# The low part of block 2's mixer weights: a subtraction, or a transfer that adds onto the negated high part

## The chip, the cores and the metric

The kernel runs on one core of one Trainium2 chip. A core has five engines with a queue each, worked off strictly in order: TensorE (PE: matmuls, and PEld: its weight loads), VectorE (DVE), ScalarE (ACT), GpSimd (POOL) and SyncE (SP). SP, ACT and POOL can issue DMA transfers; engines wait for each other by semaphores. The metric is the device time of one execution in microseconds (us), lower is better.

## The reference

The reference runs three transformer blocks over 512 tokens of width 1024 in float32. The change touches the mixers of the second block, which has two layers:

```python
for layer in range(DEPTH_2):
    h = rms_norm(x, g_mix[layer])
    proj = jnp.einsum('bsd,dc->bsc', h, w_in[layer])
    qa, ka, va, iq, ik, iw, qb, kb, vb = jnp.split(proj, split_points, axis=-1)
    # rotary embedding of qa, ka, iq, ik, qb, kb
    # dsa_mixer(qa, ka, va, iq, ik, iw) and diff_mixer(qb, kb, vb, ...), side by side
    # x += their outputs @ w_out[layer]; then a gated feed-forward part
```

The sparse mixer (dsa) scores all keys for each query with eight small index heads, keeps the 128 largest scores of each query, and attends over those keys alone; the differential mixer (diff) subtracts one softmax map from another. All products are in float32.

## The kernel before

**Exact products in two parts.** TensorE takes a reduced form of float32 (fp32r). Each operand is therefore split into a high part, its rounded value, and a low part, the rest, and a product is made of three matmuls: high by high, high by low, low by high (`mm3`, lines 348 to 352, where the weights stand still and 512 tokens stream by; lines 333 to 335 in `tok_steps`, where the tokens stand still and the weights' columns stream by).

**A piece of weights.** `load_piece` (lines 276 to 285) brings [128, n] of a weight, n up to 1024 columns: SP issues the transfer into `wraw` (four buffers), ACT casts it into `whi` (line 283), and DVE subtracts the high part from the weights into `wlo` (line 284); `whi` and `wlo` have three buffers each. A new cast into a buffer waits until TensorE has done the products of the piece three before. A piece of 1024 columns in `mm3` gives TensorE 24 matmuls.

**A layer of block 2** (`block2`, lines 880 to 1126) runs in these stages, at these times in the first layer's profile. The entrance (672 to 740 us): three index pieces of the weight `win`, each followed by the rotary embedding; then `wtA` (three pieces of 792, 792 and 528 columns; the values of half the sparse heads and the index weights, all four token tiles at once); then the first pair of query and key pieces of `win`, while the index scores (tiles `is` and `isc`, lines 927 to 942) are made. The selection stretch (740 to 840): DVE picks the largest scores eight at a time (`top8`, lines 922 to 925, tiles `m` and `isc`), TensorE does `wtC` (four pieces, the differential mixer's values) and the units of attention. The plan of attention (to 960): a written string, PLAN, sets the order of head pairs and query tiles; at each step `feed` puts a few matmuls of the coming projections in between (the other 14 query and key pieces, then `wtB`, two pieces, the values of the other sparse heads, then half of `wout` in eight pieces of 512 columns). The rest of `wout` and the feed-forward part follow.

**The rotary embedding** (`rope`, lines 867 to 878) is made for 19 tiles of a layer: ACT copies the product out of PSUM (line 871) and issues transfers that swap the halves of each head (line 874, ACT's queue), POOL multiplies by one table (line 875), DVE by the other (line 876), POOL adds (line 877).

**The order of the work.** A scheduler takes the program and writes each engine's queue from its own estimate of durations; an engine then works its queue in that order. So an instruction that moves to another engine changes the places of others too.

In what follows `p` is a product's PSUM tile, `is` and `s` the index and attention scores, `rope` the buffers of the embedding, `stile` a softmax tile.

Of the kernel before, what the change touches and what calls it, by code (L numbers as in the profile page):

```python
# [12 lines left out]
F32 = mybir.dt.float32  # L13
F32R = mybir.dt.float32r
I32 = mybir.dt.int32
AF = mybir.ActivationFunctionType
ALU = mybir.AluOpType
# [3 lines left out]
P = 128  # L21
# [9 lines left out]
# ---------------------------------------------------------------- host layout  # L31
def kpieces(w):
    """[K, M] -> [M/128, 128, K/128 * 128]: one block of columns per row, the contraction on partitions."""
    k, m = w.shape
    a = w.reshape(k // P, P, m // P, P).transpose(2, 1, 0, 3)
    return np.ascontiguousarray(a).reshape(m // P, P, k)


def kmajor(w):
    """[K, N] -> [128, K/128 * N]."""  # L40
    k, n = w.shape
    return np.ascontiguousarray(w.reshape(k // P, P, n).transpose(1, 0, 2)).reshape(P, -1)


def colvec(v):
    """[n * 128] -> [128, n]."""
# [24 lines left out]
def prep(i):  # L71
# [22 lines left out]
    # block 1  # L94
# [43 lines left out]
    # block 2  # L138
# [31 lines left out]
    # block 3  # L170
# [27 lines left out]
# ---------------------------------------------------------------- device code  # L198
class Build:
    def __init__(self, tc, aps, offs, ctx):  # L200
        self.tc, self.nc, self.aps, self.offs = tc, tc.nc, aps, offs
        self.ctx = ctx
        self.uid = 0
        self.sb = ctx.enter_context(tc.tile_pool(name="sb", bufs=1))
# [15 lines left out]
    def t512(self, dt=F32, name="t"):  # L220
        """A [128, 512] slot, taken in program order and given back with free()."""
# [15 lines left out]
    def set_ring(self, **kinds):  # L237
        """Slots that short-lived tiles of a kind go round; 0 gives them back."""
# [13 lines left out]
    def banks(self, **kinds):  # L252
        """Which PSUM banks each kind of product goes round."""
# [22 lines left out]
    # weights: one DMA of [128, n <= 1024], then the exact two-part split  # L276
    def load_piece(self, ap):
        nc = self.nc
# [7 lines left out]

    def split(self, src, name="s", tiles=None):
        """src [128, n] F32 (SBUF or PSUM) -> hi, lo."""
# [6 lines left out]
    def lin_T(self, ap, xs, tag="mm", piece=None):  # L295
        """ap [128, K] (one block of 128 output rows); xs: list of (hi, lo) per k-tile -> PSUM [128, 512]."""
        return last_of(self.lin_steps(ap, xs, tag, piece))

    def lin_steps(self, ap, xs, tag="mm", piece=None):
        """lin_T, a k-tile a step; the last step gives the result."""  # L300
# [16 lines left out]
    def tok_steps(self, ap, n, xs, done, wide=1):  # L317
        """ap [128, 8 * n]: tokens on partitions, PSUM [128, n] per token tile to done(tt, ps)."""
# [22 lines left out]
    def scaled(self, o, scale, name):  # L341
        """o * scale in two parts."""
# [4 lines left out]
    def mm3(self, out, w, x, start=True, stop=True):  # L347
        """out (+)= w.T @ x, either operand in two parts."""
# [5 lines left out]
    def scores(self, q, k, qt, masks, mx, sm):  # L354
        """Per half: exp(max - (q.k + mask)) with its row sums; q carries the turned sign."""
# [19 lines left out]
    def turned(self, t, qt):  # L375
        """[queries, keys] -> the blocks of keys on partitions, [128, block, 128 queries]."""
# [10 lines left out]
    def rsqrt(self, y, v, pool=False):  # L387
        """y = v ** -0.5 on small [128, n] tiles; v is SBUF and positive."""
# [17 lines left out]
    def bcast_cols(self, col_of_tt, tag="at"):  # L406
        """[128 tokens, 128 (broadcast)] stationary per token tile -> PSUM [128, 512] rows."""
# [5 lines left out]
    def bcast_pairs(self, cols, tag="at"):  # L413
        """cols [128 tokens, 4, 2] -> PSUM [128 = (2, 64), 512]."""
# [4 lines left out]
    # sums of squares of the residual stream, and what follows from them  # L419
# [19 lines left out]
    def col_sums(self, *accs):  # L439
        """-> PSUM [128 tokens, 4]: sums over the partitions."""  # L440
# [9 lines left out]
    def stat_end(self, st):  # L450
        """-> [128 tokens, 4]: 1 / rms"""
# [13 lines left out]
    def norm_in(self, x, g, hi, lo):  # L465
        """hi + lo = x * g, g a per-partition column."""
# [6 lines left out]
    # ------------------------------------------------------------ block 1  # L473
    def block1(self, x, B, first, g_next, stats):
# [36 lines left out]
        # the overlapping windows of the compressed keys and values, position pairs on partitions  # L511
# [99 lines left out]
        # relative bias strips, sign turned: strip[p, h, c] = -bias[bucket(p + 384 - c)], masked where negative  # L611
# [30 lines left out]
        # the two halves of the spatial gating unit, in parts that go between others  # L642
# [28 lines left out]
        # q / k norms per head  # L671
# [16 lines left out]
        # compressed branch probabilities, transposed to [(r, n), q]  # L688
# [1057 lines left out]
```

## Time and profile before

| | |
|---|---|
| Time, median of 3 runs | 3123.69 us (3121.01 to 3126.1) |
| Span of the profiled execution | 3123.8 us (nothing around it is shown) |
| Mean granted TensorE clock | 0.979 of full speed |
| TensorE, VectorE, ScalarE, GpSimd busy | 3052.9, 1785.8, 1231.4, 440.5 us |
| Casts into `whi`, whole kernel | 528, 495.5 us on ACT |
| Subtractions into `wlo`, whole kernel | 528, 599.9 us on DVE |

A profile is read from the whole to the part: the share of busy time says which engine could be the bound, windows say in which stage it is, and the chain of waits says which instruction was the last that something waited for in that stage. Idle time of an engine that is not the bound costs nothing, and an engine busy 57% of the span can still be the bound of a stage.

### The profile page before, as it was taken

What the parts mean: (1) busy time and instruction counts of PE and PEld (TensorE: products, weight loads), DVE (VectorE), ACT (ScalarE), POOL (GpSimd) and SP (SyncE); (2) the same over time, 40 slices, a digit from 0 to 9 for tenths busy, and PEclk for the clock granted to TensorE, in tenths of its full rate; (3) what the DMA queues carried; (4) which work ended last, traced back from release to release, by engine and by line L of the source; (5) the groups of instructions that cost most, each with busy time, mean ns of one, the idle gap of its engine ahead of it and who ended that gap; (6) DMA issues with size and microseconds to landing.
All of it is one profiled execution on the core that took longest, in us unless ns stands there. A gap on an engine that the chain in (4) does not pass through costs nothing.

```text
span 3123.8 us, 40875 instructions
## 1 busy us (share of the span) xinstructions
PE 3052.9 (98%) x15416; PEld 2437.1 (78%) x15416; DVE 1785.8 (57%) x3400; ACT 1231.4 (39%) x2261; POOL 440.5 (14%) x411
## 2 busy tenths in 40 slices
PE   8999999999999999999999999999999999999998
PEld 6867888887677888887677888877777888888886
DVE  6576655647976333348866333369874665543333
ACT  4365433434455222234454222347543433322222
POOL 0001000011221101121211101110820000211011
PEclk9999999998999999998899999999999999999999
DMA  5402223332212223332213233236434222322322
GB/s 175 125 22 77 90 80 109 99 100 81 74 52 92 95 81 108 97 99 80 72 47 99 93 91 102 79 107 199 155 99 155 85 86 88 108 95 78 110 83 74
DMA packets 124052, 299.95 MB, mean 96 GB/s; under 512 B 28440, under 2 KB 40792, under 8 KB 123856
## 3 DMA queue, kind: packets, MB, share of 16 engines
q1 hardware_dynamic: 115696, 285.79, 29.2%
q10 hardware_dynamic: 7680, 9.97, 1.2%
q8 instruction: 122, 2.00, 0.3%
q0 software_dynamic: 480, 1.57, 0.1%
q14 instruction: 74, 0.61, 0.1%
HBM read 272.52 MB, written 14.79 MB: 92 GB/s over the span
## 4 chain that ended last, share of the span: by engine, by line
PE 87%; DVE 6%; DMA 2%; ACT 2%; POOL 1%; issue 1%; ACTq 1%; SPq 0%; DVEq 0%; POOLq 0%
PE p L350 24%; PE p L351 24%; PE p L352 24%; PE s L362 2%; DMA rope<-rope 2%; PE tr L382 1%; PE ss L444 1%; PE p L333 1%; ACTq L874 1%; DVE isc L925 1%; PE O L1036 1%; PE p L335 1%; PE p L334 1%; POOL rope L877 1%; DVE m L924 1%
## 5 line engine op out<-in xcount | busy, mean ns | idle before, releaser
L350 PE MATMUL p<-xh,whi 128*128 128x512 f32 x2360 | 955.4, 405 | 10.6 <-ACT xh L467 7.2
L283 ACT CAST whi<-wraw 128x1024 fp32r<-128x1024 f32 (+4 forms) x528 | 495.5, 940 | 1181.3 <-PE p L351 851.5
L351 PE MATMUL p<-xl,whi 128*128 128x512 f32 x2360 | 949.4, 402 | 0.5 <-DVE xl L468 0.5
L352 PE MATMUL p<-xh,wlo 128*128 128x512 f32 x2360 | 946.5, 401 | 1.1 <-DMA wraw<-in_b_cw1k 1.1
L284 DVE TENSOR_TENSOR wlo<-wraw,whi 128x1024 fp32r<-128x1024 f32 (+4 forms) x528 | 599.9, 1138 | 325.1 <-ACT whi L283 311.9
L350 PEld LDWEIGHTS p<-xh,whi 128*128 128x128 f32 x2360 | 448.4, 190 | 120.9 <-issue 8.8
L352 PEld LDWEIGHTS p<-xh,wlo 128*128 128x128 f32 x2360 | 447.5, 190 | 107.5 <-issue 4.8
L351 PEld LDWEIGHTS p<-xl,whi 128*128 128x128 f32 x2360 | 448.2, 190 | 103.1 <-issue 5.0
L350 PE MATMUL p<-acth,whi 128*128 128x512 f32 x704 | 277.8, 395 | 0.0
L352 PE MATMUL p<-acth,wlo 128*128 128x512 f32 x704 | 277.7, 394 | 0.0
L351 PE MATMUL p<-actl,whi 128*128 128x512 f32 x704 | 277.5, 394 | 0.0
L1612 POOL TENSOR_TENSOR g<-g,rbc 128x512 f32<-128x512 f32 x66 | 114.0, 1728 | 808.5 <-ACT g L1611 808.5
L436 POOL TENSOR_TENSOR sqacc<-sqacc,sq 128x512 f32<-128x512 f32 x63 | 97.4, 1550 | 777.0 <-ACT sq L434 776.8
L1614 DVE TENSOR_TENSOR g<-g,p 128x512 f32<-128x512 f32 x66 | 45.4, 688 | 238.7 <-PE p L352 238.7
L352 PEld LDWEIGHTS p<-acth,wlo 128*128 128x128 f32 x704 | 132.2, 188 | 31.6
L351 PEld LDWEIGHTS p<-actl,whi 128*128 128x128 f32 x704 | 132.2, 188 | 31.5
L350 PEld LDWEIGHTS p<-acth,whi 128*128 128x128 f32 x704 | 132.2, 188 | 31.3
L1610 DVE TENSOR_TENSOR g<-p,rbc 128x512 f32<-128x512 f32 x66 | 45.7, 692 | 188.1 <-PE p L352 188.1
L369 ACT ACTIVATE stile<-stile,sm 128x128 f32<-128x128 f32 (+3 forms) x192 | 106.8, 557 | 83.3 <-DVE sm L366 72.1
L1634 DVE TENSOR_TENSOR x<-x,p 128x512 f32<-128x512 f32 x96 | 66.0, 688 | 108.1 <-PE p L352 107.9
L333 PE MATMUL p<-whi,xh 128*128 128x256 f32 (+2 forms) x352 | 104.6, 298 | 0.3 <-ACT rope L871 0.3
L334 PE MATMUL p<-wlo,xh 128*128 128x256 f32 (+2 forms) x352 | 102.9, 293 | 0.0
(457 smaller groups left out, 4183.4 us busy)
## 6 DMA issues: line engine op xcount, KB each, us to landing
wraw<-in_b_wup SPq DMA_DIRECT2D x176, 512.0 KB, 3.3
wraw<-in_b_win SPq DMA_DIRECT2D x118, 512.0 KB, 3.6
wraw<-in_b_wdn SPq DMA_DIRECT2D x64, 512.0 KB, 3.5
wraw<-in_b_wout SPq DMA_DIRECT2D x48, 256.0 KB, 2.7
wraw<-in_b_wdn SPq DMA_DIRECT2D x64, 192.0 KB, 2.3
rope<-rope ACTq DMA_DIRECT2D x128, 64.0 KB, 2.3
row<-rows SPq DMA_DIRECT2D x32, 256.0 KB, 4.4
wraw<-in_b_wtC SPq DMA_DIRECT2D x8, 512.0 KB, 4.0
```

Source lines behind the costliest of these rows:

```text
L283: nc.scalar.copy(hi, raw)
L284: nc.vector.tensor_tensor(lo, raw, hi.bitcast(F32), op=ALU.subtract)
L333: mm(ps, xs[k][0][:, ts], wh[:, s], start=k == 0, stop=False)
L334: mm(ps, xs[k][0][:, ts], wl[:, s], start=False, stop=False)
L350: mm(out, w[0], x[0], start=start, stop=False)
L351: mm(out, w[0], x[1], start=False, stop=False)
L352: mm(out, w[1], x[0], start=False, stop=stop)
L362: self.nc.tensor.matmul(out[g][:, :n], q[i][hs, qt * P : n], k[j][hs, :n], start=c == 0, stop=c == 2)
L369: nc.scalar.activation(t[:, :n], t[:, :n], AF.Exp, bias=mx[:, g : g + 1], scale=-1.0, accum_out=sm[:, g : g + 1])
L436: eng.tensor_tensor(accs[i], accs[i], sq, op=ALU.add)
L1612: nc.gpsimd.tensor_tensor(g, g, rbc, op=ALU.mult)
L1634: nc.vector.tensor_tensor(x[m], x[m], ps, op=ALU.add)
```

## The change

From block 2's start until its mixers are done, `load_piece` takes another way: 36 pieces a layer, 72 in all (19 of `win`, three of `wtA`, four of `wtC`, two of `wtB` and eight of `wout`'s 512-column halves in each layer). The transfer into `wraw` and the cast stay. ACT then writes the negated high part into `wlo`, and POOL issues a second transfer of the same weights from HBM which adds them onto what stands in `wlo`. The 72 subtractions of DVE go. ACT gets 72 instructions more and POOL 72 transfers of up to 512 KB. Line numbers after the change are 13 to 17 higher, since comments went.

```diff
+        self.rmw = False
...
     def load_piece(self, ap):
+        if self.rmw:
+            return self.load_piece_rmw(ap)
         nc = self.nc
...
+    def load_piece_rmw(self, ap):
+
+        nc = self.nc
+        n = ap.shape[1]
+        raw = self.t([P, 1024], tag="wraw", bufs=self.WR, name="wraw")[:, :n]
+        nc.sync.dma_start(raw, ap)
+        hi, lo = (self.t([P, 1024], tag=tg, bufs=self.WS, dt=F32R, name=tg)[:, :n] for tg in ("whi", "wlo"))
+        nc.scalar.copy(hi, raw)
+        nc.scalar.activation(lo, hi.bitcast(F32), AF.Copy, scale=-1.0)
+        nc.gpsimd.dma_start(lo, ap, accum_op=ALU.add)
+        return hi, lo
...
         self.set_ring(stile=6, pts=5, rope=4)
+        self.rmw = True
...
         self.set_ring(stile=0, pts=0, rope=0)
+        self.rmw = False
```

The scheduler writes the queues anew. In the entrance of the first layer ACT's queue stood like this before (1342, 1345: the second and third piece of `wtA`; 1348, 1356: the first query and key piece; 1325: the third index tile's embedding):

```order
L871 COPY rope_1325_6235<-p_1324_6210 128x512
L283 CAST whi_1345_6348<-wraw_1344_6346 128x528
L874 DMA rope_1326_6236<-rope_1325_6235 16x512 x3
L291 CAST idxh_1319_6200<-rope_1317_6186 128x512
L874 DMA rope_1326_6236<-rope_1325_6235 16x512 x5
L912 ACTIVATE vA_1329_6253<-p_1334_6258,rcol_1296_6073 128x256
L912 ACTIVATE vA_1330_6254<-p_1335_6259,rcol_1296_6073 128x256
L912 ACTIVATE vA_1331_6255<-p_1336_6260,rcol_1296_6073 128x256
L912 ACTIVATE vA_1332_6256<-p_1337_6261,rcol_1296_6073 128x256
L283 CAST whi_1348_6386<-wraw_1347_6384 128x1024
L283 CAST whi_1356_6431<-wraw_1355_6429 128x1024
```

and after:

```order
L886 COPY rope_1325_6238<-p_1324_6213 128x512
L298 ACTIVATE wlo_1343_6311<-whi_1342_6310 128x792
L889 DMA rope_1326_6239<-rope_1325_6238 16x512 x4
L306 CAST idxh_1319_6202<-rope_1317_6188 128x512
L889 DMA rope_1326_6239<-rope_1325_6238 16x512 x4
L297 CAST whi_1345_6353<-wraw_1344_6351 128x528
L297 CAST whi_1348_6392<-wraw_1347_6390 128x1024
L298 ACTIVATE wlo_1346_6354<-whi_1345_6353 128x528
L298 ACTIVATE wlo_1349_6393<-whi_1348_6392 128x1024
L297 CAST whi_1356_6438<-wraw_1355_6436 128x1024
```

The negations stand behind the copy and the embedding's transfers, and the cast of the third piece moved behind those transfers.

POOL's queue at the same place held only the embeddings' multiplications and additions before:

```order
L875 TENSOR_TENSOR rope_1309_6137<-rope_1309_6137,tab_1301_6094 128x512
L877 TENSOR_TENSOR rope_1309_6137<-rope_1309_6137,rope_1310_6138 128x512
L875 TENSOR_TENSOR rope_1317_6186<-rope_1317_6186,tab_1301_6094 128x512
L877 TENSOR_TENSOR rope_1317_6186<-rope_1317_6186,rope_1318_6187 128x512
L875 TENSOR_TENSOR rope_1325_6235<-rope_1325_6235,tab_1301_6094 128x512
L877 TENSOR_TENSOR rope_1325_6235<-rope_1325_6235,rope_1326_6236 128x512
```

and after (1340, 1343, 1346: `wtA`; 1349, 1357: the first query and key piece):

```order
L299 DMA wlo_1340_6268<-in_b20_wtA 128x792
L890 TENSOR_TENSOR rope_1309_6138<-rope_1309_6138,tab_1301_6094 128x512
L892 TENSOR_TENSOR rope_1309_6138<-rope_1309_6138,rope_1310_6139 128x512
L299 DMA wlo_1343_6311<-in_b20_wtA 128x792
L890 TENSOR_TENSOR rope_1317_6188<-rope_1317_6188,tab_1301_6094 128x512
L892 TENSOR_TENSOR rope_1317_6188<-rope_1317_6188,rope_1318_6189 128x512
L890 TENSOR_TENSOR rope_1325_6238<-rope_1325_6238,tab_1301_6094 128x512
L299 DMA wlo_1346_6354<-in_b20_wtA 128x528
L892 TENSOR_TENSOR rope_1325_6238<-rope_1325_6238,rope_1326_6239 128x512
L299 DMA wlo_1349_6393<-in_b20_win 128x1024
L299 DMA wlo_1357_6439<-in_b20_win 128x1024
```

The transfer of `wtA`'s third piece stands behind the multiplication for the third index tile, those of the query and key pieces behind its addition.

TensorE used the second piece of `wtA` high part and low part in turn before (after the first piece's products on three of four token tiles):

```order
L333 MATMUL p_1336_6260<-whi_1339_6264,xh_1240_5784 128x264
L334 MATMUL p_1336_6260<-wlo_1340_6265,xh_1240_5784 128x264
L335 MATMUL p_1336_6260<-whi_1339_6264,xl_1241_5785 128x264
L333 MATMUL p_1334_6258<-whi_1342_6306,xh_1250_5838 128x264
L334 MATMUL p_1334_6258<-wlo_1343_6307,xh_1250_5838 128x264
L335 MATMUL p_1334_6258<-whi_1342_6306,xl_1251_5839 128x264
L333 MATMUL p_1334_6258<-whi_1342_6306,xh_1260_5892 128x264
```

and after:

```order
L349 MATMUL p_1337_6264<-wlo_1340_6268,xh_1220_5677 128x264
L350 MATMUL p_1337_6264<-whi_1339_6267,xl_1221_5678 128x264
L348 MATMUL p_1337_6264<-whi_1339_6267,xh_1230_5730 128x264
L349 MATMUL p_1337_6264<-wlo_1340_6268,xh_1230_5730 128x264
L350 MATMUL p_1337_6264<-whi_1339_6267,xl_1231_5731 128x264
L348 MATMUL p_1337_6264<-whi_1339_6267,xh_1240_5784 128x264
L349 MATMUL p_1337_6264<-wlo_1340_6268,xh_1240_5784 128x264
L350 MATMUL p_1337_6264<-whi_1339_6267,xl_1241_5785 128x264
L348 MATMUL p_1337_6264<-whi_1342_6310,xh_1250_5838 128x264
L349 MATMUL p_1334_6261<-wlo_1343_6311,xh_1250_5838 128x264
L350 MATMUL p_1334_6261<-whi_1342_6310,xl_1251_5839 128x264
L348 MATMUL p_1334_6261<-whi_1342_6310,xh_1260_5892 128x264
```

It now does all 36 products of the first piece and four with the second piece's high part before the first that needs its low part, 40 in all.

At `wtB`'s second piece (1777 and 1778) ACT's queue after the change is this; before, the cast stood alone, some 16 us ahead of its use:

```order
L297 CAST whi_1777_8159<-wraw_1776_8157 128x1024
L482 ACTIVATE qh_1736_7995<-rope_1734_7985 128x512
L399 COPY pts_1750_8045<-tr_1749_8040 128x512
L384 ACTIVATE stile_1761_8094,sm_1757_8084<-stile_1761_8094,sm_1756_8083 128x384
L384 ACTIVATE stile_1762_8097,sm_1757_8084<-stile_1762_8097,sm_1756_8083 128x384
L1016 ACTIVATE osq_1585_7425,sm_1584_7424<-O_1648_7668 128x128
L399 COPY pts_1764_8109<-tr_1763_8107 128x128
L886 COPY rope_1765_8114<-p_1741_8006 128x512
L298 ACTIVATE wlo_1778_8160<-whi_1777_8159 128x1024
L889 DMA rope_1766_8115<-rope_1765_8114 32x512 x4
```

The negation stands eight instructions behind its cast, after the copy into `rope_1765`. TensorE there, before and after:

```order
L334 MATMUL p_1772_8115<-wlo_1775_8119,xh_1250_5838 128x256
L335 MATMUL p_1772_8115<-whi_1774_8118,xl_1251_5839 128x256
L333 MATMUL p_1772_8115<-whi_1777_8136,xh_1260_5892 128x256
L334 MATMUL p_1772_8115<-wlo_1778_8137,xh_1260_5892 128x256
L335 MATMUL p_1772_8115<-whi_1777_8136,xl_1261_5893 128x256
```

```order
L350 MATMUL p_1789_8206<-whi_1774_8140,xl_1251_5839 128x256
L348 MATMUL p_1789_8206<-whi_1777_8159,xh_1260_5892 128x256
L377 MATMUL s_1793_8231<-kh_1609_7543,qh_1601_7497 128x512
L377 MATMUL s_1794_8232<-kh_1609_7543,qh_1601_7497 128x512
L377 MATMUL s_1793_8231<-kl_1610_7544,qh_1601_7497 128x512
L1031 MATMUL oT_1769_8128<-pack_13_85,ob_1755_8081 128x128 x4
L349 MATMUL p_1772_8137<-wlo_1778_8160,xh_1260_5892 128x256
L350 MATMUL p_1772_8137<-whi_1777_8159,xl_1261_5893 128x256
```

The low part was used right after the high part; now other products stand in between.

## Rows read from the trace of the kernel before

Times are microseconds from the span's start; a group's row gives its busy time and the mean of one in ns, then the idle time before it and what ended it.

**Rows 1.** Section 1 of the page: busy us, share of the span, instructions.

```profile
PE 3052.9 (98%) x15416; PEld 2437.1 (78%) x15416; DVE 1785.8 (57%) x3400; ACT 1231.4 (39%) x2261; POOL 440.5 (14%) x411
```

**Rows 2.** Groups by line, 692 to 980 us: busy, mean ns; idle before.

```profile
L283 ACT CAST whi<-wraw 128x1024 fp32r<-128x1024 f32 x22 | 22.9, 1048 | 14.3 <-PE p L351 13.2 <-PE p L335 0.9
...
L284 DVE TENSOR_TENSOR wlo<-wraw,whi 128x1024 fp32r<-128x1024 f32 (+3 forms) x35 | 41.2, 1187 | 18.7 <-ACT whi L283 16.8 <-PE p L352 1.9
```

**Rows 3.** Chain by line, 692 to 980 us.

```profile
by line: PE p L350 9.7%; DMA rope<-rope 9.1%; PE p L351 8.8%; PE p L352 8.0%; PE s L362 7.5%; DVE isc L925 4.2%; PE O L1036 4.0%; issue 4.0%; DVE m L924 3.8%; POOL rope L877 3.6%; PE tr L382 3.4%; ACTq L874 2.9%; DVE wlo L284 2.9%; DVE rope
```

**Rows 4.** Windows, first layer: length; PE, PEld, DVE, ACT, POOL busy (count); clock, DMA share, GB/s.

```profile
692.00:740.00 48.00, 43.80 (x256) 36.67 (x254) 24.20 (x30) 16.47 (x31) 15.57 (x11) 0.90 0.39 114
...
757.00:840.00 83.00, 76.35 (x411) 61.06 (x409) 77.22 (x211) 37.08 (x92) 19.93 (x21) 0.94 0.28 83
```

**Rows 5.** Chain by line, 757 to 840 us (selection stretch, first layer).

```profile
by line: DVE isc L925 14.4%; DVE m L924 13.3%; DVE wlo L284 8.4%; DVE rope L876 5.9%; issue 5.9%; DMA rope<-rope 5.9%; POOL rope L877 5.7%; DVE stile L366 4.9%; PE s L362 4.7%; PE p L350 4.3%; PE p L351 4.2%; DVE stile L986 4.0%; PE p L352 
```

**Rows 6.** Chain pieces by time, same stretch: start, us, what.

```profile
759.29 2.35 DVE wlo L284 x2
...
813.82 1.14 DVE wlo L284
```

**Rows 7.** Chain by line, 1450 to 1532 us (selection stretch, second layer).

```profile
by line: DVE isc L925 14.1%; DVE m L924 12.9%; DMA rope<-rope 10.6%; POOL rope L877 7.3%; DVE wlo L284 7.1%; issue 6.5%; PE s L362 6.0%; DVE stile L366 4.5%; DVE rope L876 4.2%; ACTq L874 3.2%; PE p L350 2.4%; DVE stile L986 2.3%; PE p L352
```

**Rows 8.** DMA issues: count, KB each, median us from issue to landing.

```profile
wraw<-in_b_win SPq DMA_DIRECT2D x118, 512.0 KB, 3.6
...
wraw<-in_b_wout SPq DMA_DIRECT2D x48, 256.0 KB, 2.7
...
sys<-dAT POOLq DMA_DIRECT2D x2, 256.0 KB, 6.4
dT<-sys POOLq DMA_DIRECT2D x2, 256.0 KB, 3.7
```

**Rows 9.** Timeline of ACT, cast of the layer's first index piece.

```profile
671.78 1.05 ACT L283 CAST whi<-wraw 128x1024 fp32r<-128x1024 f32 x1 [1.59 <-PE p L351]
```

**Rows 10.** Timeline of PE, that piece's first products.

```profile
680.78 0.39 PE L352 MATMUL p<-xh,wlo 128*128 128x512 f32 x1
```

**Rows 11.** Timeline of PE, entrance to the first query product.

```profile
698.93 0.28 PE L333 MATMUL p<-whi,xh 128*128 128x264 f32 x1
699.06 0.29 PE L334 MATMUL p<-wlo,xh 128*128 128x264 f32 x1
...
716.00 0.69 PE L352 MATMUL p<-xh,wlo 128*128 128x512 f32 x1
716.48 0.63 PE L350 MATMUL p<-xh,whi 128*128 128x512 f32 x1
...
720.87 0.40 PE L350 MATMUL p<-xh,whi 128*128 128x512 f32 x1
```

**Rows 12.** Timeline of ACT, entrance: start, us, instruction [idle before].

```profile
694.77 0.86 ACT L283 CAST whi<-wraw 128x792 fp32r<-128x792 f32 x1
...
702.99 0.59 ACT L871 COPY rope<-p 128x512 f32<-128x512 f32 x1 [2.56 <-DMA rope<-rope]
```

**Rows 13.** Timeline of POOL, entrance.

```profile
712.96 1.79 POOL L875 TENSOR_TENSOR rope<-rope,tab 128x512 f32<-128x512 f32 x1 [4.65 <-DMA rope<-rope]
714.83 2.14 POOL L877 TENSOR_TENSOR rope<-rope,rope 128x512 f32<-128x512 f32 x1
```

**Rows 14.** Line 1287, a transfer issued by POOL: ns min/median/max of the issue.

```profile
L1287 POOL DMA_DIRECT2D sys<-dAT x2: 547/634/720, 2192.6 to 2193.3; - x2
```

**Rows 15.** Timeline of ACT, copy near the second piece of wtB.

```profile
879.62 0.59 ACT L871 COPY rope<-p 128x512 f32<-128x512 f32 x1
```

**Rows 16.** Timeline of PE, first product with the low part of wtB's second piece.

```profile
879.98 0.28 PE L334 MATMUL p<-wlo,xh 128*128 128x256 f32 x1
```

**Rows 17.** Timeline of ACT, cast of the fourth piece of wtC.

```profile
757.71 1.03 ACT L283 CAST whi<-wraw 128x1024 fp32r<-128x1024 f32 x1
```

**Rows 18.** Timeline of PE, first product with that piece.

```profile
759.84 0.40 PE L333 MATMUL p<-whi,xh 128*128 128x256 f32 x2
```

## The prediction

> **What bounds the kernel now.** I read the page's busy times first, then the windows of one mixer layer, then the chain in each window, and last the timelines where a piece of weights is used soon after it is made. TensorE is busy 98% of the span and VectorE 57% [rows 1], so over the whole span a VectorE instruction is free unless its own stage waits for it. The 72 subtractions that go sit in the two mixers of block 2, so I looked there. Between 692 and 980 us VectorE does 35 of them in 41.2 us [rows 2], and the chain through that stretch holds 2.9% of wlo, 8 us, against 9.1% of the rope's transfers, 26 us [rows 3]. In the stretch from 757 to 840 us, where VectorE picks the 128 largest index scores of each query, VectorE is busy 77.22 of 83 us and TensorE 76.35 [rows 4]: there VectorE sets the pace. The chain of that stretch names wlo with 8.4%, 7.0 us [rows 5]; these are six subtractions in five places [rows 6]. The same stretch of the second layer has 7.1% of 82 us, 5.8 us [rows 7]. In the entrance, 692 to 740 us (the products with wtA, the index scores and the first query and key), TensorE idles 4.2 us and its granted clock is 0.90 [rows 4].
>
> **What goes.** 72 subtractions, of which 7.0 + 5.8 us stand on the chain [rows 5, 7]. The most that VectorE's relief could give in the selection stretch is its whole idle time and lost clock: 83 - 76.35 = 6.65 us idle and, of 83 us at 0.94, 5 us of clock, together 11.6 us a layer; the least is nothing. I take the chain's figure, since the subtraction's place is taken by the next VectorE instruction and nothing else ends late there.
>
> **What comes: the way of a piece.** Before, the low part follows the cast by one VectorE instruction of 1.2 us [rows 2]. After, it needs a negation on ScalarE and then a transfer. The trace has no such activation; the cast of the same shape on the same engine takes 1.05 us [rows 2], which I take. It has no accumulating transfer either. POOL issued transfers of 256 KB that landed in 3.7 to 6.4 us, where SP's of that size land in 2.7 and SP's of 512 KB in 3.6 [rows 8]: POOL's cost 1 to 3.7 us more. So a plain one of 512 KB would take 4.6 to 7.3 us. I take 6.5, in the upper half, because this one must also read its target. The ends I keep are 3 (no dearer than SP's) and 10 (its 3.6 doubled, plus POOL's 3 or so).
>
> The Trainium skill ("DMA: Bandwidth & Descriptors", section "Anatomy of one DMA — SWDGE (gpsimd) path") gives 2.0 us plus bytes over 436e3 for a transfer issued by GpSimd, which is 2.6 us for 256 KB and 3.2 for 512 KB. This trace has 3.7 and 6.4 for 256 KB [rows 8], so the measured rows decide; by the page the sum below would come to about +5 us and not +23.
>
> Between the cast and the first product with the low part most pieces have 9 us or more, because three buffers of each part let the cast run two pieces ahead (24 matmuls of 0.23 us a piece, so 11 us). Needed are 1.05 + 6.5 = 7.6 us. The layer's first index piece is such a one: cast ended at 672.83, low part used at 680.78, 7.95 us [rows 9, 10]. These, about 30 of 36, I cost at nothing; the cover is gone at a transfer of 6.9 us for this one. What is left are pieces that are used at once, and pieces that the new order delays.
>
> **Entrance.** TensorE starts wtA at 698.93 and issues a matmul every 0.12 us [rows 11]. The new order lets it do 40 matmuls before it needs the low part of the second piece: 703.7 us. That piece's negation stands behind the copy into the rope's buffer, which ends at 702.99 + 0.59, later by 0.86 for the first piece's negation; its own 0.86 follows [rows 12]: 705.3, landed at about 711.4 (396 KB, so 0.4 less than 6.5). TensorE waits 7.7 us. The third piece's transfer waits on POOL for the rope's multiplication (712.96 + 1.79), and the one for the first query piece also for the rope's addition, 2.14 us [rows 13]; with 0.6 us an issue [rows 14] the latter goes out at about 718.4 and lands at 725, where TensorE used that low part at 716.00 before [rows 11]. So 9 us later at that place, the stall of 7.7 being inside. One microsecond I take off for products that TensorE now does ahead: +8. With a transfer of 3 us it is +5, with 10 it is +12.
>
> **Clock.** After the idle time at this place before, matmuls took 0.63 us where the same ones take 0.40 later [rows 11], and the granted clock of the window is 0.90 [rows 4]. A wait of 8 us within wtA brings a second such piece of about 6 us at the lower of its two levels (1.2 in place of 2.4 GHz), in which some 3 us are lost: +3 (0 to +4).
>
> **wtB and wtC.** The negation of wtB's second piece moves behind a copy that ends at 880.21 [rows 15], so it ends at 881.3 and lands at 887.8. TensorE used it at 879.98 [rows 16] and now has 3.2 us of other products ahead, until 883.2: +5 (+1 at 3 us, +8 at 10). wtC's fourth piece is cast from 757.71 [rows 17], negated by 759.8, landed at 766.3; its products started at 759.84 [rows 18], and 38 matmuls of 0.12 us now go between the first with its high part and the first with its low part, plus the first wait: 765.2. +1 (0 to +4.5).
>
> **Rope.** Its transfers share the engines with 18 MB a layer more; 26 us of them are on the chain [rows 3]. I put +1 (0 to +6, a quarter longer). ScalarE takes 36 negations a layer more, 22.9 us for the 22 of full width [rows 2], and has room for them even in the selection stretch, where it is busy 37 of 83 us [rows 4].
>
> **Sum.** First layer 8 + 3 + 5 + 1 + 1 - 7.0 = +11; second, of the same build, 18 - 5.8 = +12. Together +23 us. The durations come from one profiled execution, whose span is 3123.8 us; the page gives no time around it, and the median of the runs is 3123.69, 0.1 us off: 3147 us.
>
> **Rivals.** (A) Faster: VectorE's relief gives the full 11.6 us a layer, since TensorE idles in that stretch for VectorE alone, and the entrance hides its delay, because there TensorE idles 4.2 us already [rows 4]. It decides if the transfer lands in about 3.5 us. Then the entrance costs +1, wtB +2, and a layer gains 8.6: 3107 us. For it: the chain names VectorE lines first in that stretch [rows 5]. Against it: POOL's landed transfers [rows 8]. (B) No change: at 3 to 4 us the entrance costs 5, the clock 1, wtB 2, and the relief gives 8: 3124 us. (C) Much slower: the transfer takes 9.5 us. Then 3 us more stand at each of three places (entrance, wtB, wtC), 2.6 at the start [rows 9, 10] and 2 of clock: 13.6 a layer more, 3174 us. For it speaks that an accumulation moves its target twice. The Trainium skill has a rule for that ("Collectives: The Full Stack", section "The bandwidth ceiling: the fold count and why AG ≠ RS ≠ AR"): a reducing transfer reads two sources for each write, and ran at about half the rate of a plain one. No row here shows it.
>
> **How the numbers follow.** Forecast 0.45, A 0.20, B 0.15, C 0.20. A measurement of this kernel tells changes above 0.2%, 6.2 us. A lies on the faster side, B within, the forecast and C on the slower: faster 0.20, same 0.15, slower 0.65. The forecast's own range is 3134 to 3160. The whole range, 3108 to 3185, takes in B and nearly all of A and C.
>
> **What would show it.** In the profile of the changed kernel: the landing of wlo's transfers from POOL (6.5 us; under 4 speaks for A or B, over 8 for C); TensorE's longest wait within wtA, by a product with wlo, of 6 to 9 us, and one at wtB's second piece; a lower granted clock in the entrance; the selection stretch 6 to 7 us shorter, with no VectorE line for wlo on its chain. I am wrong if the stretch shortens by over 10 us, if TensorE waits for wlo at most pieces, or if the rope's transfers double.

## The result

| | us |
|---|---|
| Kernel before, median of 4 runs | 3124.89 (3121.01 to 3129.21) |
| Changed kernel, median of 4 runs | 3173.33 (3166.52 to 3175.97) |
| Ratio | 1.0153, 95% interval 1.0138 to 1.0169 |
| Forecast | 3147 (3108 to 3185) |

The change costs 48.4 us, where 23 were forecast: the right side, and just over twice the size. It is inside the range, at the price of rival C (3174), but by luck: C's reason did not come true, as will be seen.

**Where the time went.** The same instructions of both profiles were set against each other. Work after the first layer's mixers runs 30.6 us later, of which 1.9 were there before the block began; work after the second layer's runs 50.0 us later. So the first mixer costs 28.7 us, the second 19.3, and the rest of the kernel about nothing. By the same instructions the first mixer loses 10.0 us in the entrance (692 to 740 us before), 3.4 in the selection stretch (757 to 840), 12.1 between 840 and 900 and 2.4 after that; the second loses 9 in the entrance, 7.7 in the selection stretch and 2.7 after it. These are the windows of each mixer, with the same TensorE instructions in each, of before:

```profile
660.00:1000.00 340.00, 323.51 (x1781) 251.73 (x1779) 244.19 (x597) 158.76 (x364) 71.55 (x66) 0.94 0.26 78
1330.00:1680.00 350.00, 333.50 (x1821) 259.75 (x1820) 243.00 (x596) 156.89 (x362) 69.19 (x63) 0.94 0.25 75
```

and of the changed kernel (columns as in [rows 4]: length; PE, PEld, DVE, ACT, POOL busy; clock; DMA share; GB/s):

```profile
661.90:1030.60 368.70, 341.50 (x1781) 263.93 (x1779) 207.09 (x561) 187.99 (x400) 99.02 (x102) 0.90 0.49 116
1360.60:1730.00 369.40, 340.75 (x1821) 264.94 (x1820) 206.90 (x560) 185.99 (x398) 98.33 (x99) 0.93 0.49 115
```

VectorE is relieved as meant, by 37 and 36 us, and ScalarE takes 29 more in each layer. TensorE idles 27.2 and 28.7 us in place of 16.5 and 16.5: 10.7 and 12.2 us more. The rest is that the same matmuls are busy for 18.0 and 7.3 us longer, and most of that is the clock: length times (1 - granted clock) is 20 and 21 us before, 37 and 26 after. The DMA engines' share nearly doubles, from 0.26 to 0.49, while the bytes rise by half only, from 78 to 116 GB/s.

**The rows that answer to those of before.** Section 1 of the page [rows 1]:

```profile
PE 3076.9 (97%) x15416; PEld 2453.8 (77%) x15416; DVE 1705.7 (54%) x3328; ACT 1290.6 (41%) x2333; POOL 499.0 (16%) x483
```

DMA issues [rows 8], KB each and median us to landing; before, the embedding's exchange:

```profile
rope<-rope ACTq DMA_DIRECT2D x128, 64.0 KB, 2.3
...
rope<-rope ACTq DMA_DIRECT2D x48, 32.0 KB, 2.0
```

and after:

```profile
wlo<-in_b_win POOLq DMA_DIRECT2D x38, 512.0 KB, 5.8
...
rope<-rope ACTq DMA_DIRECT2D x128, 64.0 KB, 2.5
wlo<-in_b_wtC POOLq DMA_DIRECT2D x8, 512.0 KB, 6.7
wlo<-in_b_wout POOLq DMA_DIRECT2D x16, 256.0 KB, 4.4
...
rope<-rope ACTq DMA_DIRECT2D x48, 32.0 KB, 2.7
```

The accumulating transfer lands in 5.8 us; 6.5 was taken. The exchange, `rope<-rope`, takes a little longer. The negation and POOL's issue (ns, min/median/max):

```profile
L298 ACT ACTIVATE wlo<-whi x72: 630/1052/1087, 675.8 to 1708.3; 128x1024 fp32r<-128x1024 f32 x50, 128x512 fp32r<-128x512 f32 x16, 128x792 fp32r<-128x792 f32 x4, 128x528 fp32r<-128x528 f32 x2
```

```profile
L299 POOL DMA_DIRECT2D wlo<-in_b_win x38: 848/870/1191, 677.3 to 1656.7; - x38
```

TensorE's waits in the first layer (total us, times, longest):

```profile
PE p L349 <- DMA wlo<-in_b_wtA: 5.4, 2, 4.5
PE p L349 <- DMA wlo<-in_b_wtC: 3.4, 1, 3.4
PE s L377 <- ACT kh L306: 3.4, 2, 2.8
PE p L367 <- DMA wlo<-in_b_win: 2.7, 1, 2.7
...
PE p L349 <- DMA wlo<-in_b_wtB: 2.1, 1, 2.1
```

TensorE waits for a low part five times, 13.6 us in all, at the places the forecast named. And the chain by line of the selection stretch, 770 to 858 us, which answers to [rows 5]:

```profile
by line: DMA rope<-rope 12.5%; issue 11.8%; DMA wlo<-in_b_wtC 8.5%; PE s L377 8.5%; PE p L365 7.5%; PE p L367 7.5%; PE p L366 7.0%; POOL rope L892 4.5%; DVE isc L941 4.1%; POOL rope L890 3.4%; ACTq L889 3.1%; DVE m L940 2.9%; PE p L349 2.5%
```

This is the row to read twice. VectorE's search, `isc` and `m`, led the chain with 27.7% and holds 7.0% now, so VectorE no longer sets the pace. But the embedding's exchange went from 5.9% of 83 us to 12.5% of 88, from 4.9 to 11 us, and the transfer of `wtC`'s low part brings 7.5. The stretch did not get shorter; its bound changed hands. Over the whole first mixer, though, the chain (662 to 1031 us) has no more of the exchange than before:

```profile
by line: PE p L365 11.3%; PE p L367 11.0%; PE p L366 10.6%; issue 7.8%; PE s L377 7.5%; DMA rope<-rope 6.2%; DMA wlo<-in_b_win 3.8%; PE tr L397 3.3%; ACTq L889 3.3%; PE O L1052 3.2%; POOL rope L892 2.8%; POOL rope L890 2.5%; PE p L349 2.2%;
```

That is 23 us of exchange where [rows 3] had 26. What grew there are the low parts: their negations, issues and transfers stand with 31 us on this chain, where the subtractions had 8; in the second layer with 33, where they had 6. A chain follows only what ended last, so the experiments must say what each of the two is worth.

How one embedding and the low parts get into each other's way is seen on POOL in the entrance (start, us, instruction, idle before it):

```profile
699.38 1.82 POOL L890 TENSOR_TENSOR rope<-rope,tab 128x512 f32<-128x512 f32 x1 [5.89 <-DMA rope<-rope]
701.28 1.30 POOL L892 TENSOR_TENSOR rope<-rope,rope 128x512 f32<-128x512 f32 x1
707.46 0.87 POOL L299 DMA_DIRECT2D wlo<-in_b_wtA  x1 [4.88 <-ACT wlo L298]
708.07 1.56 POOL L890 TENSOR_TENSOR rope<-rope,tab 128x512 f32<-128x512 f32 x1
709.70 1.26 POOL L892 TENSOR_TENSOR rope<-rope,rope 128x512 f32<-128x512 f32 x1
715.96 1.80 POOL L890 TENSOR_TENSOR rope<-rope,tab 128x512 f32<-128x512 f32 x1 [5.00 <-DMA rope<-rope]
717.71 0.89 POOL L299 DMA_DIRECT2D wlo<-in_b_wtA  x1
718.31 1.59 POOL L892 TENSOR_TENSOR rope<-rope,rope 128x512 f32<-128x512 f32 x1
```

The transfer at 707.46 waited for its negation, with the embedding's multiplication of 708.07 behind it; the transfer at 717.71 stood behind a multiplication that waited for the exchange. The chain of the entrance names these pieces in order of time (start, us, what):

```profile
705.09 1.96 DMA rope<-rope
...
708.07 1.57 POOL rope L890
...
712.85 2.86 DMA rope<-rope
...
717.71 0.14 POOL wlo L299
...
718.31 0.92 POOL rope L892
...
719.54 8.34 DMA wlo<-in_b_win
...
727.93 0.50 PE p L367
```

The exchange had landed at 707.05, so the multiplication of 708.07 was held 1 us. The transfer for the first query piece goes out at 719.54, where 718.4 was forecast, but beside the other transfers it takes 8.34 us, and TensorE has that low part at 727.9 in place of 716.0 [rows 11].

### The profile page after: what moved, and what is told of

The parts are those of the page before. It is cut to its first block, busy times and chain, and to the rows that moved or that the text cites. A ratio compares the mean times of both kernels' runs of the same rounds, so it can differ in the third digit from the quotient of the medians.

```text
span 3171.4 us, 40997 instructions
## 1 busy us (share of the span) xinstructions
PE 3076.9 (97%) x15416; PEld 2453.8 (77%) x15416; DVE 1705.7 (54%) x3328; ACT 1290.6 (41%) x2333; POOL 499.0 (16%) x483
## 3 DMA queue, kind: packets, MB, share of 16 engines
q0 software_dynamic: 10848, 34.15, 6.2%
## 4 chain that ended last, share of the span: by engine, by line
PE 83%; DMA 4%; DVE 4%; POOL 4%; issue 2%; ACT 2%; ACTq 1%; SPq 0%; POOLq 0%; DVEq 0%
PE p L365 23%; PE p L367 23%; PE p L366 23%; PE s L377 2%; DMA rope<-rope 1%; PE tr L397 1%; PE p L349 1%; PE p L350 1%; POOL sys L1320 1%; PE p L348 1%; POOL subst L1315 1%; PE ss L459 1%; DMA wlo<-in_b_win 1%; ACTq L889 1%; PE O L1052 1%
## 5 line engine op out<-in xcount | busy, mean ns | idle before, releaser
L286 ACT CAST whi<-wraw 128x1024 fp32r<-128x1024 f32 (+3 forms) x456 | 428.9, 941 | 1134.3 <-PE p L366 811.1
L287 DVE TENSOR_TENSOR wlo<-wraw,whi 128x1024 fp32r<-128x1024 f32 (+3 forms) x456 | 508.1, 1115 | 278.2 <-ACT whi L286 268.8
L349 PE MATMUL p<-wlo,xh 128*128 128x256 f32 (+2 forms) x352 | 109.8, 313 | 24.9 <-DMA wlo<-in_b_wtA 11.8
```

The lines of the kernel that those rows point to most:

```text
L286: nc.scalar.copy(hi, raw)
L287: nc.vector.tensor_tensor(lo, raw, hi.bitcast(F32), op=ALU.subtract)
L349: mm(ps, xs[k][0][:, ts], wl[:, s], start=False, stop=False)
```

## The experiments

Eighteen kernels were run, each beside the kernel before. Differences are of medians. The ratio is worked out from all runs and not from the two medians; by it e1's -13.2 us is -10.6, from -14.1 to -6.9.

| run | us | before | difference | ratio, 95% interval |
|---|---|---|---|---|
| e1_negation_only | 3112.48 | 3125.69 | -13.2 | 0.9966 (0.9955 to 0.9978) |
| e2_early_only | 3153.67 | 3125.69 | +28.0 | 1.0093 (1.0073 to 1.0113) |
| e3_plan_only | 3138.97 | 3125.69 | +13.3 | 1.0049 (1.0036 to 1.0062) |
| e4_second_transfer | 3164.21 | 3125.69 | +38.5 | 1.0124 (1.0109 to 1.0139) |
| e5_second_load_by_sp | 3133.98 | 3120.94 | +13.0 | 1.0036 (1.0022 to 1.0050) |
| e6_small_second_transfer | 3123.13 | 3120.94 | +2.2 | 1.0001 (0.9984 to 1.0017) |
| e7_small_add | 3131.45 | 3120.94 | +10.5 | 1.0027 (1.0012 to 1.0041) |
| e8_pool_subtracts | 3142.51 | 3120.94 | +21.6 | 1.0061 (1.0044 to 1.0079) |
| e9_before_no_exchange | 3122.65 | 3126.45 | -3.8 | 0.9985 (0.9971 to 0.9998) |
| e10_after_no_exchange | 3116.26 | 3126.45 | -10.2 | 0.9966 (0.9953 to 0.9979) |
| e11_second_transfer_no_exchange | 3138.77 | 3126.45 | +12.3 | 1.0040 (1.0025 to 1.0054) |
| e12_second_transfer_plain | 3148.14 | 3126.45 | +21.7 | 1.0075 (1.0056 to 1.0095) |
| e13_after_exchange_by_sp | 3162.20 | 3127.40 | +34.8 | 1.0112 (1.0093 to 1.0131) |
| e14_before_exchange_by_sp | 3113.72 | 3127.40 | -13.7 | 0.9956 (0.9940 to 0.9972) |
| e15_after_exchange_by_copies | 3151.71 | 3127.40 | +24.3 | 1.0075 (1.0057 to 1.0093) |
| e16_before_exchange_by_copies | 3137.96 | 3127.40 | +10.6 | 1.0037 (1.0021 to 1.0052) |
| e17_after_embedding_on_vector | 3119.39 | 3124.25 | -4.9 | 0.9986 (0.9977 to 0.9996) |
| e18_before_embedding_on_vector | 3117.56 | 3124.25 | -6.7 | 0.9979 (0.9966 to 0.9991) |

**e1: the relief by itself.**

```diff
         nc.scalar.activation(lo, hi.bitcast(F32), AF.Copy, scale=-1.0)
-        nc.gpsimd.dma_start(lo, ap, accum_op=ALU.add)
```

> The changed kernel without the accumulating transfers: the low part stays the negated high part, so the weights themselves are not added (left out: that addition, in all 72 pieces). Theory W (waits): the loss comes from about 14 pieces a layer that are used soon after they are made, whose low part now lands late, and from the lower TensorE clock after those waits. Then without the transfers nothing is late, ScalarE has the time, and only VectorE's relief is left: 10 to 20 us under the kernel before, about 3105 to 3115. Theory T (traffic): the second transfer of 33 MB and POOL's time for it slow the rotary embedding's transfers; it expects the same here. Theory O (order): the loss comes from the new order of ScalarE's and TensorE's queues, with 72 negations ahead of other work; it expects 10 us or more above the kernel before.

It was 13.2 us faster. So the relief is real, about 6.6 us a layer, and neither the negations nor the new order costs more than it gives: theory O is out. The transfers, with the waits for them, make the other 62 us between it and the changed kernel.

**e2 and e3: which pieces.**

```diff
 e2, before the plan's projections (wtB's steps set it again):
+        self.rmw = False
         fill = filling()
 e3: lin_steps gets a piece loaded the new way, all else the old:
+        self.rmw = True
+        piece = self.load_piece(ap)
+        self.rmw = False
```

> The new way for 14 of 36 pieces a layer alone (three index pieces, wtA, the first query and key, wtC, wtB); the 22 others keep the subtraction. Theory W expects nearly the whole loss, +40 to +50 us against the kernel before (3165 to 3175), the gain on the plan's pieces being missing. Theory T expects the share of the bytes, 28 of 72 pieces, about +19 (3143). Theory O expects about half, +20 to +25.

> The new way for the other 22 pieces a layer alone (14 query and key pieces of the plan, eight of wout); index pieces, wtA, wtB, wtC and the first query and key keep the subtraction. Theory W expects no loss, and a gain of up to 10 us from VectorE's relief in the selection stretch: 3114 to 3126. Theory T expects the larger share of the bytes, +25 to +29 (3150). Theory O expects +20 to +25.

No theory fits. The 14 early pieces cost 28 us, where W expected 40 to 50 and T 19; the 22 others, for which TensorE hardly waits (no low part is among its ten largest waits in the first layer), cost 13, where W expected a gain and T at least 25. Together they make 41 of the 48 us.

**e4: transfers that nobody's product waits for.**

```diff
         nc.vector.tensor_tensor(lo, raw, hi.bitcast(F32), op=ALU.subtract)
+        if self.extra:
+            nc.gpsimd.dma_start(raw, ap, accum_op=ALU.add)
```

> The kernel before, with its subtractions, and in addition POOL's 72 accumulating transfers of the same bytes, onto the raw weights once they have been read; nothing is computed from them, the next load into that buffer alone waits. Theory W expects 0 to +6 us (3124 to 3130). Theory T expects most of the loss, +25 to +48. Theory O expects about nothing.

+38.5 us, with every subtraction in its place and the low parts as early as before. Theory W, on which the forecast was built, cannot carry the loss alone: this much of it needs no late low part. In its trace TensorE waits longest for the keys that come out of the embedding and for the index scores (first layer; these rows were 6.6 and 2.7 us before, so they make 5 of the 24 us that this layer is longer):

```profile
PE s L365 <- ACT kh L294: 9.7, 5, 3.2
PE is L353 <- ACT relu L944: 4.6, 4, 1.9
```

**e5, e6, e12: bytes, queue, adding.**

```diff
 e5:  nc.sync.dma_start(raw, ap)
+     if self.extra:
+         nc.sync.dma_start(raw, ap)
 e6, in e4's place:
+     nc.gpsimd.dma_start(raw[:, :16], ap[:, :16], accum_op=ALU.add)
 e12, in e4's place:
+     nc.gpsimd.dma_start(raw, ap)
```

> The kernel before, in which SP loads each of the 72 pieces twice into the same buffer before the cast: the bytes of the second transfer without POOL and without an accumulation. The run with POOL's second transfer and the old subtractions was 38 us slower. Theory T (the transfers share the engines with the rotary embedding's, which come late): +20 to +38 us. Theory Q (POOL's queue: 72 issues and the waits for their pieces stand in front of the embedding's multiplications and additions): 0 to +5.

> The kernel before with POOL's 72 accumulating transfers onto the raw weights, of 16 columns (8 KB) in place of up to 1024 (512 KB): as many issues and waits on POOL, as many rows in each transfer, hardly any bytes. Theory T: 0 to +8 us. Theory Q: +20 to +38.

> The kernel before with subtractions and POOL's 72 second transfers onto the raw weights, plain ones that do not add. With adding it was +38 us, as second loads by SP +11. If the adding itself, which holds the DMA engines nearly twice as long for a byte, makes the difference: +8 to +18 us. If it is that POOL issues them, at a place of its own behind the subtraction: +30 to +38.

POOL's issues and waits without the bytes cost nothing that can be told (e6, whose 72 issues are as long: 0.87 us). The bytes without POOL cost 13 us (in e5 the cast waits for the second load too, so this is not the bytes alone), bytes by POOL 22, bytes by POOL with adding 38. The page's DMA section shows in what the last two differ (packets, MB, share of 16 engines' span); e12, then e4:

```profile
q0 software_dynamic: 9440, 34.15, 3.5%
```

```profile
q0 software_dynamic: 10848, 34.15, 6.0%
```

For the same 34.15 MB the adding transfers held the engines 1.7 times as long. The Trainium skill ("Collectives: The Full Stack", section "The bandwidth ceiling: the fold count and why AG ≠ RS ≠ AR") puts a reduce step, which reads two sources for each write, at about half the rate of a copy. These two rows come near it.

What this does to the embedding was taken from the timelines: for all 38 embeddings of both layers, the time from ScalarE's copy to the end of POOL's addition was summed. It is 418.7 us before; 1.8 more in e6, 9.3 in e5, 22.3 in e12, 39.4 in e4. The kernels were 2.2, 13.0, 21.7 and 38.5 us slower. In these four, which differ from before in a second transfer alone, what the embeddings lose is nearly what the kernel loses. In the changed kernel they lose 40.5 us. This is one trace for each kernel, and the match does not hold where the low parts go the new way for some pieces or with few bytes: the embeddings lose 12.9 us in e2 and the kernel 28.0, 27.8 in e3 and the kernel 13.3, and in e7 they gain 16.8 while the kernel loses 10.5.

**e7 and e8: a small addition, and another place for the subtraction.**

```diff
 e7:
-        nc.gpsimd.dma_start(lo, ap, accum_op=ALU.add)
+        nc.gpsimd.dma_start(lo[:, :16], ap[:, :16], accum_op=ALU.add)
 e8 (self.pool holds for the query and key pieces of units 1 to 4):
-        nc.vector.tensor_tensor(lo, raw, hi.bitcast(F32), op=ALU.subtract)
+        (nc.gpsimd if self.pool else nc.vector).tensor_tensor(lo, raw, hi.bitcast(F32), op=ALU.subtract)
```

> The changed kernel with the accumulating transfer cut to 16 of a piece's columns (left out: the weights' addition in the other columns). All 72 negations, issues and waits stay; the transfers land sooner and move 1 MB in place of 33. Theory W (the late landing at the pieces used soon): near the run without transfers, -13 to -3 us against the kernel before, with waits on wlo of under 2 us. Theory T: the same, -13 to -3. Theory Q: +5 to +25.

> The kernel before, with the subtraction of the eight query and key pieces of units 1 to 4 in each layer on POOL in place of VectorE, and no second transfer: an attempt to get VectorE's relief in the selection stretch (13 us without any transfer, over all pieces) for less. If VectorE sets the pace there and POOL has room: 3 to 8 us faster than before. If POOL's queue matters (theory Q: the embedding's work waits behind subtractions of 3 us or more): 0 to +10.

e7 is 38 us below the changed kernel, so bytes make most of the loss there too; but it is 24 above e1. Its transfers land in 2.2 to 2.7 us, and still TensorE waits for `wtA`'s low part, 7.9 us in the first layer: that is the place in the queues, not the size. So theory W keeps a part: 24 us for the places and waits (e7 against e1) and 38 for bytes (e4) make the 62 us between e1 and the changed kernel. e8 missed: the kernel was 21.6 us slower. POOL took 2.4 us for each of the 16 subtractions, and the selection stretches are 9.4 and 10.7 us longer. That the embeddings wait behind the subtractions is not shown: their sum is 414.1 us, 4.6 less than before.

**e9 to e11: without the exchange.**

```diff
-        for p in range(0, P, dim):
-            for a, b in ((p, p + dim // 2), (p + dim // 2, p)):
-                nc.scalar.dma_start(t[a : a + dim // 2], o[b : b + dim // 2])
...
-        nc.vector.tensor_tensor(t, t, sn, op=ALU.mult)
+        nc.vector.tensor_tensor(t, ps, sn, op=ALU.mult)
```

> The kernel before without the rotary embedding's transfers, the baseline of the two runs after it: VectorE multiplies the product itself in place of its exchanged halves (left out: the exchange of halves). 15 to 45 us faster than before, since 26 us of a layer's chain are these transfers.

> The changed kernel with the same cut (left out: the exchange of halves). Against the baseline without exchange: theory T (the second transfers delay the embedding's) expects +5 to +20 us, what the late low parts cost less VectorE's relief. Theory W (the late landing of the low parts) expects +35 to +50 as with the exchange.

> The kernel before with subtractions and POOL's 72 accumulating transfers onto the raw weights, which was 38 us slower than before, with the same cut (left out: the exchange of halves). Theory T: 0 to +8 us against the baseline without exchange. If the second transfers harm by another way (the raw buffers come free late, SP's loads come late): +20 to +38.

Without the exchange the change makes the kernel 6.4 us faster (e10 against e9), where it made it 48.4 slower. e4's transfers cost 16.1 (e11 against e9) in place of 38.5. So most of the loss needs the exchange. What makes e11's 16.1 us was not found; its embeddings take 183 us where e9's take 157, though none waits for an exchange. e9 itself missed: the exchange stands with 26 us on a layer's chain, and taking it away gave 3.8 in all.

**e13 to e16: whose queue.**

```diff
 e13, e14:
-                nc.scalar.dma_start(t[a : a + dim // 2], o[b : b + dim // 2])
+                nc.sync.dma_start(t[a : a + dim // 2], o[b : b + dim // 2])
 e15, e16, for heads of 64:
+                    nc.scalar.copy(t[a : a + 32], ps[b : b + 32])
```

> The changed kernel with the embedding's exchange transfers issued by SP in place of ScalarE; nothing is left out. Theory T (the transfers share the engines): still +30 to +48 us against the same edit of the kernel before. Theory A (the negations stand behind the issues in ScalarE's queue): at most +15 against it.

> The kernel before with the exchange transfers issued by SP: the baseline of the run above. Within 10 us of the kernel before either way: ScalarE loses 2.5 us of issues for each embedding, but SP's loads and these transfers now stand in one queue.

> The changed kernel in which ScalarE makes the exchange of the 64-wide heads by four copies out of PSUM, 32 partitions each, in place of the transfers (16 of 19 embeddings a layer; the index heads keep the transfers); nothing is left out. Theory T: -6 to +8 us against the same edit of the kernel before. Theory A: ScalarE stays as busy, so +25 to +48 against it. It is also a try for a version faster than both.

> The kernel before with the exchange of the 64-wide heads by ScalarE's copies: the baseline of the run above. The wait for the transfers is 5 to 7 us in the entrance and 2.4 us of copies take its place: 5 to 15 us faster than the kernel before, less if VectorE sets the pace anyway (without any exchange it was 4 us).

With the exchange issued by SP the change costs 48.5 us (e13 against e14), as much as ever, so ScalarE's issues are not the way and theory A is out. With 16 of 19 exchanges made by copies it costs 13.8 (e15 against e16). By the number of exchanges through transfers: 19, 48 us; three, 14; none, -6. e14 is the fastest kernel here that computes all, 13.7 us faster than before. ScalarE no longer holds its queue for 176 issues of 0.6 us; that this is the reason was not tested.

**e17 and e18: the embedding off POOL.**

```diff
-        nc.gpsimd.tensor_tensor(o, o, cs, op=ALU.mult)
+        nc.vector.tensor_tensor(o, o, cs, op=ALU.mult)
...
-        nc.gpsimd.tensor_tensor(o, o, t, op=ALU.add)
+        nc.vector.tensor_tensor(o, o, t, op=ALU.add)
```

> The changed kernel with the embedding's multiplication by the cosines and its addition on VectorE in place of POOL; nothing is left out. Against the same edit of the kernel before: +30 to +50 us if the shared engines alone do the harm (theory T), 0 to +15 if POOL's queue does (theory Q2: the accumulating transfers wait there behind multiplications that wait for the exchange).

> The kernel before with the embedding's multiplication and addition on VectorE: the baseline of the run above. VectorE does each in about 0.7 us where POOL takes 1.3 to 2.1, but it sets the pace in the selection stretch, 38 instructions a layer more: between 10 us faster and 25 us slower than the kernel before.

The change now costs 1.8 us, which these runs do not tell from nothing. In e17 the exchange lands as late as ever in a kernel with the second transfers:

```profile
wlo<-in_b_win POOLq DMA_DIRECT2D x38, 512.0 KB, 5.6
rope<-rope ACTq DMA_DIRECT2D x128, 64.0 KB, 3.1
...
rope<-rope ACTq DMA_DIRECT2D x48, 32.0 KB, 3.2
```

In e18 it lands in 2.0 and 2.5 us. From the end of ScalarE's copy to the last landing in the trace the 38 exchanges take 256 us in e17 and 196 in e18, so the delay by the second transfers is still there. The embeddings' sum, to the last of their instructions, is nevertheless shorter in e17, 415.8 us for 444.1: all embeddings together, VectorE, which the change relieves, begins its first step 41 us after these landings in e17 and 112 in e18. By the same instructions e17 loses 5.5 us in the first layer's entrance and 4.4 in its selection stretch, and wins 12.1 between 840 and 900 us. So the pair does not clear the shared engines, theory T: VectorE's relief can be worth more where VectorE does the embedding, and pay for the loss. e4's transfers on e18, which relieve nobody, would have told, and were not run.

**What is shown, and what stays open.** Shown: the second transfers cost 38.5 us though no product waits for them (e4); it is their bytes (e6), and their adding makes it worse (e12 against e4); most of it needs the exchange (16.1 of 38.5 are left in e11, and the change costs nothing in e10); ScalarE's issues are not the way (e13, e14). Shown too: 24 us of the changed kernel's loss are there with transfers of 8 KB (e7 against e1). The traces divide what the embeddings lose. From the end of ScalarE's copy to the last landing the 38 exchanges take 241 us before, 271 in e4 and 268 in the changed kernel; from there to POOL's multiplication it is 10, 21 and 17. So of some 40 us the exchange landing later makes 30 and 26, and POOL's queue 11 and 7. These sums are rough: about one landing in eight is missing in each trace, and e6, which moves hardly any bytes more, has 226 in place of 241. Open are e11's rest, and whether the embedding must be on POOL for the loss, which e17 and e18 leave undecided.

## Why the prediction was half wrong

The forecast's sum was -13 us for what goes and +36 for what comes. The runs give -13 (e1), +24 for the places in the queues and the waits behind them (e7 against e1) and +38 for the bytes (e4, and the changed kernel against e7). So the places and waits were priced too high, at 34, and the bytes, at 2 of the 36, far too low.

- **The way of a piece**: right. Negation 1.05 us as taken, landing 5.8 for 6.5 taken.
- **Entrance, wtB, wtC**: the places were right and the sizes near. The longest wait in `wtA` was 4.5 us, not 7.7; `wtB` 2.1, not 5; `wtC` 3.4, not 1; all five waits for low parts 13.6 us in the first layer. The entrance is 10.0 us longer by the same instructions, where +8 and +3 of clock were forecast. That the numbers meet is in part luck: in e4, where no product waits for a low part from a transfer, the same stretch is 10.8 us longer.
- **Rope, "+1 (0 to +6, a quarter longer)"**: this step failed. It stands for all that the second transfers do to others, 2 us in two layers, and e4 measured that at 38.5. The embeddings are 24 and 16 us longer in the two layers. The forecast had the row for it, 26 us a layer on the chain [rows 3], and priced the sharing by bytes alone (18 MB a layer, where it is 16.3); that adding holds the engines 1.7 times as long is not in this term. It saw the transfers waiting behind POOL's multiplications [rows 13], but not the multiplications waiting behind the transfers.
- **What goes, "nothing else ends late there"**: failed. e1 gives the relief at 13.2 us, and 12.8 were taken. In the changed kernel the first layer's selection stretch is 3.4 us longer and not 6 to 7 shorter, with the exchange and `wtC`'s low part on its chain in VectorE's stead.
- **Clock, "+3 (0 to +4)"**: mis-sized, and at another place. The same matmuls were busy 18.0 and 7.3 us longer, but in the first layer's entrance the mean granted clock only went from 0.89 to 0.88. The longest stretch at the lower level came after two waits of 0.8 and 2.3 us at 849 and 858 us, both ended by VectorE's instructions of attention:

```profile
860.00:868.00 8.00, 7.21 (x26) 4.48 (x26) 4.18 (x17) 3.39 (x10) 2.29 (x3) 0.62 0.52 104
868.00:876.00 8.00, 8.00 (x27) 4.91 (x26) 3.47 (x13) 3.21 (x11) 0.84 (x2) 0.50 0.30 57
876.00:884.00 8.00, 8.00 (x22) 5.45 (x21) 5.20 (x16) 3.74 (x11) 0.79 (x2) 0.50 0.07 16
```

  The clock is the third number from the end: 0.62, 0.50, 0.50, about half the speed for over 20 us; the forecast had thought of one stretch of 6 us a layer. e1 has a stretch like it without any transfer: the instructions of 840 to 900 us take 67.3 us at a clock of 0.82 there, 71.5 at 0.79 in the changed kernel, 59.3 at 0.97 before. So this piece cannot be put down to the transfers alone.
- **Rivals.** C had the time and not the cause: the transfer takes 5.8 us, not 9.5. Its argument, that an accumulation moves its target too, held in another place: it lengthens the engines' time (e12 against e4), and the kernel with it. A and B needed a landing of 3 to 4 us; and by e4 the second transfer costs 38 us even if nobody waits for it.

## What to carry to other kernels

A transfer that is put in place of an instruction is priced twice: by its own landing, and by whose transfers and whose queue it gets in the way of; here the first was 24 us and the second 38. If an engine is the bound of a stage, look for what ends second in that stage before counting the gain, and whether the edit makes that one later. Of the engine that is to issue new transfers, list what else its queue holds on the path. Here, with that work on the relieved engine, the change cost 2 us in place of 48: the exchange's delay stayed, and time won elsewhere paid for it.

## What was not expected of the hardware

- Accumulating transfers held the DMA engines 6.0% of the span for 34.15 MB, plain ones of the same engine and bytes 3.5%. They landed in 5.6 us against 4.4 for 512 KB (e4, e12); SP's took 3.5 (e12).
- POOL was busy 0.87 us with the issue of an accumulating transfer, at 512 KB as at 8 KB (e4, e6), and 0.53 to 0.58 with a plain one (e12).
- The exchange issued by SP in place of ScalarE made the kernel before 13.7 us faster (e14).
